# Streaming the moving operand of the float32r products alternately from its two halves

## The chip, the cores and the metric

The kernel runs on one core of a Trainium2 chip. The metric is the device time of one execution in microseconds (us), first instruction to last with what the program needs around them; lower is better. TensorE multiplies, VectorE (DVE) and ScalarE (ACT) read the results and prepare operands, SyncE (SP) and GpSimd (POOL) issue the transfers from memory.

## The reference, cut to what matters

A decoder block on 512 tokens of 1024 channels, in float32:

```python
h = _rmsnorm(x, norm_mix_g)
proj = h @ w_in                       # 1024 x 9216
p_a, p_b, q, p_g = jnp.split(proj, IN_SPLITS, axis=-1)
...
y_a = (gb * _causal_dwconv(gc * v, conv_a_w)) @ w_a_out
u = u * jax.nn.sigmoid(ug)
u = _causal_dwconv(u, conv_b_w) + conv_b_bias          # 31 taps
y_b = jax.nn.silu(_layernorm(u, ln_b_g, ln_b_b)) @ w_b_out
...                                   # 4 heads over 256 memory tokens: o
y_c = o @ w_att_out
merged = g[:, :, 0] * y_a + g[:, :, 1] * y_b + g[:, :, 2] * y_c
x = x + merged @ w_o
u = _causal_dwconv(_rmsnorm(x, norm_ffn_g) @ w_up, conv_ffn_w)
gt, up = jnp.split(u, 2, axis=-1)
x = x + (jax.nn.silu(gt) * up) @ w_down
out = _rmsnorm(x, norm_final_g)
```

## The kernel before, in words

**Products in three passes.** TensorE is fed float32r, a form of float32 that it streams in one pass but with fewer bits. So every operand is split into a high part (ACT casts it, `whi`, line 495 for weights) and a low part (DVE subtracts the high part from the source, `wlo`, line 499), and each product is three matmuls: high by high, high by low, low by high, summed in PSUM. Each matmul first loads a stationary operand of 128 columns (its own instruction, PEld in the profile) and then streams the moving operand, 256 or 512 columns, one after the other as they lie in SBUF.

**Seven products instead of eight.** The large products are formed by a scheme of Strassen's kind. A "quad" is one step of it for two blocks of 256 output channels: products 1, 2, 5, 6, 7, 3, 4 (`OPERAND`, line 553), each with sums or differences of weight blocks as its weights, gathered into banks a, b, c of PSUM and read out on the way (`quad_reads`, line 694, jobs r1 to r7). One product of a quad is 24 matmuls of 256 columns (`multiply`, line 663: weights stationary, the split activations `fb00`, `ft5` and so on moving). 18 quads make the input projection and 11 the up projection. So do the product with `w_o` (line 1598) and the down projection (`steps`, line 2051), with activations stationary and 512 columns of weights moving, through `product` (line 443). The three output products of the branches (`merge_product`, line 1407) stream 512 columns of activations; keys and scores stream 256, values and weighted sums 512.

Counted from the code: 29 quads x 7 x 24 + 192 (keys) + 96 (scores) + 66 (end of the down projection) = 5226 float32r matmuls of 256 columns, and 1319 of 512, of which two (the channel mean, line 1297) do not pass through a changed line.

**Who sets the order.** PE's order is written out by hand (`seq`, lines 1771 to 1885). Every other engine's order comes from `Jobs.run` (line 229): each job has an engine, an estimated cost, the jobs it comes after and the buffers it takes. The due time of a job is worked out backwards from the estimated costs of the PE jobs (`MM`, `MM_HALF`, `MM_QUAD`, line 419, us for a matmul), moved by two tables of offsets (`LATER`, `AHEAD`), and among the ready jobs the one with the earliest start and due time is emitted next. The split weights lie in a ring of four buffers (`UNIT_BUFS`), the raw ones in six.

**Readers of the banks.** With PSUM columns in the order of the tokens, or of the output channels, ACT and DVE read a bank from front to back: `quad_reads` (lines 702 to 724), the keys (838), values (896, 904), exponentials (1082), attention output (1133, 1138), gates (`weigh`, 1451), the rows after `w_o` (`add_row`, 1629) and after the down projection (`read`, `read_end`, 2073, 2084). The reading r7 is a scalar_tensor_tensor (`minus`, line 452), which gives -a - s.

Of the kernel before, what the change touches and what calls it, by code (L numbers as in the profile page):

```python
# [331 lines left out]
def hybrid_block_kernel(  # L332
# [83 lines left out]
        return n / 1160.0 + 0.175 + extra  # L416

    TAP = 0.665
    MM, MM_HALF, MM_QUAD = 0.2268, 0.12, 0.1142
    LOAD, MORE, MORE_WIDE = 1.42, 2.55, 2.55  # L420
    LOAD_LATENCY, MORE_LATENCY = 3.1, 3.4

# [17 lines left out]
    nc.scalar.dma_start(out=pk[:, :N_GAINS], in_=packed[:, :N_GAINS])  # L440
    nc.scalar.copy(mean_w, mean_col.broadcast_to([P, P]))

    def product(ps, w_hi, w_lo, s_hi, s_lo, start, stop, again=False):


        nc.tensor.matmul(ps, s_hi, w_hi, start=start, stop=False, skip_group_check=again)  # L446
        nc.tensor.matmul(ps, s_hi, w_lo, start=False, stop=False, skip_group_check=again)  # L447
        nc.tensor.matmul(ps, s_lo, w_hi, start=False, stop=stop, skip_group_check=again)  # L448
# [214 lines left out]
    def multiply(q, f, act):  # L663
        if f in (1, 2, 5):
            make(("bank", q, BANK_OF[f]))
        ps = halves(("bank", q, BANK_OF[f]))
        (w_hi, w_lo), (hi, lo) = w_units.pop((q, f)), form[act, OPERAND[f]]
        for c in range(2):
            at = slice(c * P, (c + 1) * P)
            for i in range(4):  # L670
                k = 3 - i if f == 4 and c else i
                first = f in (1, 2, 5) and i == 0 and c == 0
                again = not (f in (1, 2, 5) and c == 0)
                for n, (w, a) in enumerate(((w_hi, hi), (w_hi, lo), (w_lo, hi))):
                    nc.tensor.matmul(  # L675
                        ps[:, c, :], w[:, k, at], a[k], start=first and n == 0,
                        stop=i == 3 and n == 2, skip_group_check=again,
                    )

# [14 lines left out]
    def quad_reads(q, first, second, ring, after=()):  # L694

        f, s = lambda: two(first), lambda: two(second)
        bank = lambda b: ("bank", q, b)
        view = lambda b: halves(bank(b))

        def read1():  # L700
            make(first)
            nc.scalar.copy(f()[:, :, lo_t], view("a"))

        def read5():
            make(second)
            nc.scalar.copy(s()[:, :, hi_t], view("b"))

        def add(t, b):
            nc.vector.tensor_tensor(t, t, b, op=ALU.add)

        job(("r1", q), "ACT", actv(512), read1, [(q, 1)] + list(after),
            take=[(first, ring)], use=[bank("a")])
        job(("r2", q), "DVE", dve(512), lambda: add(f()[:, :, lo_t], view("c")),
            [(q, 2), ("r1", q)], use=[bank("c"), first])
        job(("r5", q), "ACT", actv(512), read5, [(q, 5)] + list(after),
            take=[(second, ring)], use=[bank("b")])
        job(("r6", q), "ACT", actv(512), lambda: nc.scalar.copy(f()[:, :, hi_t], view("a")),
            [(q, 6), ("r1", q)], use=[bank("a"), first])
        job(("r7", q), "DVE", dve(512), lambda: minus(s()[:, :, hi_t], view("a"), s()[:, :, hi_t]),
            [(q, 7), ("r5", q)], use=[bank("a"), second])  # L720
        job(("r3", q), "DVE", dve(512), lambda: add(f()[:, :, hi_t], view("b")),
            [(q, 3), ("r6", q)], use=[bank("b"), first])
        job(("r4", q), "ACT", actv(512), lambda: nc.scalar.activation(
            s()[:, :, lo_t], view("a"), AF.Copy, scale=-1.0), [(q, 4), ("r5", q)],
            use=[bank("a"), second])

    def ready_of(q, second):
# [101 lines left out]
    for h in range(HEADS):  # L829
        for g in range(2):  # L830
            if h or g:
                unit_job(("K", h, g), block(w_kv, h * 256, g))

        def keys_scaled(h=h):
            make(("kt", h))
            t = tiles["kt", h][:, :512].rearrange("p (c n) -> p c n", c=2)
            row = tiles["rm",][:, :N_MEM].unsqueeze(1).broadcast_to([P, 2, N_MEM])
            nc.vector.tensor_tensor(t, halves(("bank", "K", h)), row, op=ALU.mult)
# [49 lines left out]
    for hp in range(2):  # L888
        for kp in range(4):
            if hp or kp:  # L890
                unit_job(("V", hp, kp), w_v[hp, kp], 2)
        for c in range(MC):
            def values_high(hp=hp, c=c):
                if c == 0:
                    make(("vh", hp), F32R)
                nc.scalar.activation(
                    two(("vh", hp))[:, c, :], tiles["bank", "V", hp, c], AF.Copy,
                    scale=R_MEM[:, c : c + 1],
                )

            def values_low(hp=hp, c=c):
                if c == 0:
                    make(("vl", hp), F32R)
                nc.vector.scalar_tensor_tensor(
                    two(("vl", hp))[:, c, :], tiles["bank", "V", hp, c], R_MEM[:, c : c + 1],
                    two(("vh", hp))[:, c, :].bitcast(F32), op0=ALU.mult, op1=ALU.subtract,
                )

            new = lambda s: [((s, hp), ANY)] if c == 0 else []
            old = lambda s: [] if c == 0 else [(s, hp)]  # L910
            job(("vh", hp, c), "ACT", scaled_act(512), values_high,
                [("V", hp, 3), ("m", "scale")] + ([("vh", hp, 0)] if c else []), take=new("vh"),
                use=[("bank", "V", hp, c)] + old("vh"))
            job(("vl", hp, c), "DVE", TAP, values_low,
                [("vh", hp, c)] + ([("vl", hp, 0)] if c else []), take=new("vl"),
                use=[("bank", "V", hp, c), ("vh", hp)] + old("vl"))

    def keys_product(h, g, ks):
# [6 lines left out]
        for j in range(2):  # L925
            at, again = slice(j * P, (j + 1) * P), j > 0
            for k in ks:
                for n, (w, a) in enumerate(((w_hi, m_hi), (w_hi, m_lo), (w_lo, m_hi))):
                    nc.tensor.matmul(  # L929
                        ps[:, j, :], w[:, k, at], a[:, k, :],  # L930
                        start=first and j == 0 and k == 0 and n == 0,
                        stop=g == 1 and k == 3 and n == 2, skip_group_check=again,
                    )
# [117 lines left out]
    for h in range(HEADS):  # L1051
# [18 lines left out]
        for tp in range(2):  # L1070
# [7 lines left out]
            def exps(h=h, tp=tp, top=top, den=den, bank=bank):  # L1078
                if tp == 0:
                    make(("pr", h))  # L1080
                for i in range(2):
                    nc.scalar.activation(
                        four(("pr", h))[:, 2 * tp + i, :], halves(bank)[:, i, :], AF.Exp,
                        bias=top[:, i : i + 1], accum_out=den[:, i : i + 1],
                    )

# [38 lines left out]
        for d in range(2):  # L1125
# [4 lines left out]
            def o_high(h=h, d=d, bank=bank):  # L1130
                if d == 0:
                    make(("oh", h), F32R)
                nc.scalar.copy(two(("oh", h))[:, d, :], tiles[bank])

            def o_low(h=h, d=d, bank=bank):
                if d == 0:
                    make(("ol", h), F32R)
                nc.vector.tensor_tensor(
                    two(("ol", h))[:, d, :], tiles[bank], two(("oh", h))[:, d, :].bitcast(F32),
                    op=ALU.subtract,  # L1140
                )

            job(("oh", h, d), "ACT", actv(512), o_high,
# [263 lines left out]
    def merge_product(br, m, g):  # L1407
        w_hi, w_lo = w_units.pop(("merge", br, m, g))
        for j in range(2):
# [2 lines left out]
            at = slice(j * P, (j + 1) * P)  # L1412
            for i in range(4):
                k = 4 * g + i
                hi, lo = (two((s, k // 2))[:, k % 2, :] for s in PARTS[br])
                first, last = k == 0, k == KC - 1
                nc.tensor.matmul(ps, w_hi[:, i, at], hi, start=first, stop=False)  # L1417
                nc.tensor.matmul(ps, w_hi[:, i, at], lo, start=False, stop=False)  # L1418
# [13 lines left out]
    for br in (2, 0, 1):  # L1432
        for m in range(4):
# [14 lines left out]
            for j in range(2):  # L1448
                def weigh(j=j, br=br, m=m, gate=gate):
                    t = two(gate)[:, j, :]  # L1450
                    nc.vector.tensor_tensor(t, tiles["bank", "y", br, m, j], t, op=ALU.mult)

                job(("weigh", br, m, j), "DVE", dve(512), weigh,
                    [("merge", br, m, 1), ("sigmoid", br, m)],
# [170 lines left out]

    def add_row(p, t):
        for r, h, sign in WO_READ[p]:
            row = two(("x1", 2 * r + t))[:, h, :]
            nc.vector.tensor_tensor(
                row, row, tiles["bank", "wo", wo_bank(p), t],  # L1630
                op=ALU.add if sign > 0 else ALU.subtract,
            )

# [435 lines left out]

    def read(p, t):  # L2070
        for r, h, sign in READ[p]:
            row = late["x1"][2 * r + t][h]
            nc.vector.tensor_tensor(
                row, row, tiles["bank", chain(p), t],
                op=ALU.add if sign > 0 else ALU.subtract,
            )

    def read_end(i):
# [5 lines left out]
        nc.vector.tensor_tensor(row, row, src, op=ALU.add)  # L2084

    def square(t, h, cols=slice(0, SEQ), into=None):
        nc.scalar.activation(
# [149 lines left out]
```

## Time and profile before

| What | Value |
|---|---|
| time, 3 runs | 925.33 us median (925.14 to 925.72) |
| span of the profiled execution | 923.8 us; its own time is not listed apart, and the median of the runs is 1.5 us above the span |
| PE, PEld busy | 916.6 us (6677 matmuls), 862.8 us |
| DVE, ACT, POOL busy | 837.4, 671.0, 126.5 us |
| granted TensorE clock, mean | 0.999 |
| DMA | 190.60 MB, mean 206 GB/s |

How to read the profile: busy time counts an instruction from its start to its end. Matmuls overlap, so the busy time of PE says that it always had one in flight, not how fast they went; for that the distance from one start to the next is read from the timeline, or a piece of the chain is divided by its count. The chain is followed back from the last instruction to what released it, step by step. In a group of instructions "idle before" is time that the engine stood still ahead of them, with what ended it. Tile names stand without buffer numbers: `bank<-fb10h,whi` is a matmul that writes a PSUM bank from the moving operand `fb10h` and the stationary `whi`.

### The profile page before, as it was taken

Reading aid. Unit: us, or ns where it says so; the run is one execution under the profiler, and the core shown is the slowest. Engines: PE = TensorE matmul, PEld = TensorE weight load, DVE = VectorE, ACT = ScalarE, POOL = GpSimd, SP = SyncE. Lnnn points to the kernel's source line nnn. Section 1 sums busy time; section 2 is a strip of 40 time slices with the busy share of each in tenths; the row PEclk is TensorE's granted clock in tenths of the full one; section 3 lists DMA queues with packets and bytes.
Section 4 is the critical chain, followed back from the end, with each engine's and each line's share of the span. In section 5 each row is a group of like instructions: output and inputs, shape, how many; then the busy total and the mean of one; then the engine's idle time right before and its main releaser. Section 6 shows DMA issues by size and latency. Waiting matters only on the chain.

```text
span 923.8 us, 16764 instructions
## 1 busy us (share of the span) xinstructions
PE 916.6 (99%) x6677; PEld 862.8 (93%) x6677; DVE 837.4 (91%) x953; ACT 671.0 (73%) x911; POOL 126.5 (14%) x153
## 2 busy tenths in 40 slices
PE   9999999999999999999999999999999999999997
PEld 8999999999989999999899888899999999988886
DVE  6897999989989999999986779898999889999987
ACT  7567988879977887788746743777766676765656
POOL 0121121101111211110100001021221121003300
PEclk9999999999999999999999999999999999999999
DMA  9999689666787879788956598499999877789962
GB/s 364 367 252 199 151 178 205 167 160 137 194 188 205 183 168 213 174 210 201 220 108 173 157 322 187 114 227 307 279 248 226 207 142 149 197 266 338 244 131 92
DMA packets 54366, 190.60 MB, mean 206 GB/s; under 512 B 6160, under 2 KB 6544, under 8 KB 54288
## 3 DMA queue, kind: packets, MB, share of 16 engines
q0 software_dynamic: 20880, 75.24, 45.2%
q1 hardware_dynamic: 33120, 114.02, 34.7%
q8 instruction: 52, 0.85, 0.3%
q10 hardware_dynamic: 288, 0.27, 0.1%
q14 instruction: 26, 0.21, 0.1%
HBM read 185.31 MB, written 4.19 MB: 205 GB/s over the span
## 4 chain that ended last, share of the span: by engine, by line
PE 95%; DMA 2%; DVE 1%; issue 0%; ACT 0%; POOL 0%; DVEq 0%; POOLq 0%; ACTq 0%
PE bank L675 57%; PE bank L448 7%; PE bank L446 7%; PE bank L447 7%; PE bank L1418 5%; PE bank L1417 5%; PE bank L1419 5%; PE bank L929 2%; DMA wf<-in_w_up 2%; PE bank L1766 0%; PE ss L802 0%; DVE wlo L499 0%; PE bank L1166 0%; DVE upc L1373 0%; DVE gtc L1373 0%
## 5 line engine op out<-in xcount | busy, mean ns | idle before, releaser
L495 ACT CAST whi<-wf 128x1024 fp32r<-128x1024 f32 (+1 forms) x199 | 206.9, 1044 | 97.7 <-PE bank L675 39.3
L499 DVE TENSOR_TENSOR wlo<-wf,whi 128x1024 fp32r<-128x1024 f32 (+1 forms) x193 | 232.4, 1211 | 29.8 <-ACT whi L495 29.6
L1238 ACT ACTIVATE tp<-u,pk 128x510 f32<-128x510 f32 (+22 forms) x184 | 119.4, 704 | 7.0 <-DVE acc L1245 6.9
L1245 DVE TENSOR_TENSOR acc<-acc,tp 128x1020 f32<-128x1020 f32 (+22 forms) x92 | 109.2, 1188 | 6.0 <-ACT tp L1238 5.0
L633 POOL DMA_DIRECT2D wf<-in_w_in x51 | 45.1, 890 | 245.1 <-DVE wlo L499 160.2
L675 PE MATMUL bank<-ft6h,wlo 128*128 128x256 f32 x232 | 64.3, 277 | 0.1
L675 PE MATMUL bank<-fb10h,whi 128*128 128x256 f32 x232 | 64.4, 278 | 0.0
L675 PE MATMUL bank<-fb00h,whi 128*128 128x256 f32 x232 | 64.4, 278 | 0.0
L675 PE MATMUL bank<-ft6h,whi 128*128 128x256 f32 x232 | 64.4, 277 | 0.0
L675 PE MATMUL bank<-ft7h,whi 128*128 128x256 f32 x232 | 64.3, 277 | 0.0
L675 PE MATMUL bank<-ft7l,whi 128*128 128x256 f32 x232 | 64.3, 277 | 0.0
L675 PE MATMUL bank<-ft7h,wlo 128*128 128x256 f32 x232 | 64.3, 277 | 0.0
L675 PE MATMUL bank<-fb00l,whi 128*128 128x256 f32 x232 | 64.3, 277 | 0.0
L675 PE MATMUL bank<-fb11h,whi 128*128 128x256 f32 x232 | 64.3, 277 | 0.0
L675 PE MATMUL bank<-fb00h,wlo 128*128 128x256 f32 x232 | 64.3, 277 | 0.0
L675 PE MATMUL bank<-ft5h,wlo 128*128 128x256 f32 x232 | 64.3, 277 | 0.0
L675 PE MATMUL bank<-ft5h,whi 128*128 128x256 f32 x232 | 64.3, 277 | 0.0
L675 PE MATMUL bank<-ft5l,whi 128*128 128x256 f32 x232 | 64.3, 277 | 0.0
L675 PE MATMUL bank<-ft6l,whi 128*128 128x256 f32 x232 | 64.2, 277 | 0.0
L675 PE MATMUL bank<-fb10h,wlo 128*128 128x256 f32 x232 | 64.2, 277 | 0.0
L675 PE MATMUL bank<-fb10l,whi 128*128 128x256 f32 x232 | 64.2, 277 | 0.0
L675 PE MATMUL bank<-fb11l,whi 128*128 128x256 f32 x232 | 64.1, 276 | 0.0
(388 smaller groups left out, 3146.1 us busy)
## 6 DMA issues: line engine op xcount, KB each, us to landing
wf<-in_w_in SPq DMA_DIRECT2D x55, 512.0 KB, 5.1
wf<-in_w_in POOLq DMA_DIRECT2D x51, 512.0 KB, 6.2
wf<-in_w_up SPq DMA_DIRECT2D x29, 512.0 KB, 5.7
wf<-in_w_up POOLq DMA_DIRECT2D x28, 512.0 KB, 6.1
wf<-in_w_down SPq DMA_DIRECT2D x15, 512.0 KB, 3.7
wf<-in_w_att_out SPq DMA_DIRECT2D x8, 512.0 KB, 4.5
wf<-in_w_a_out SPq DMA_DIRECT2D x8, 512.0 KB, 4.2
wf<-in_w_b_out SPq DMA_DIRECT2D x8, 512.0 KB, 4.3
```

The source lines that it names most:

```text
L446: nc.tensor.matmul(ps, s_hi, w_hi, start=start, stop=False, skip_group_check=again)
L447: nc.tensor.matmul(ps, s_hi, w_lo, start=False, stop=False, skip_group_check=again)
L448: nc.tensor.matmul(ps, s_lo, w_hi, start=False, stop=stop, skip_group_check=again)
L495: nc.scalar.copy(parts[0], src())
L499: nc.vector.tensor_tensor(lo, src(), hi.bitcast(F32), op=ALU.subtract)
L633: nc.gpsimd.dma_start(out=tiles[key], in_=block(w, col[c], k), accum_op=ALU.add)
L675: nc.tensor.matmul(ps[:, c, :], w[:, k, at], a[k], start=first and n == 0, stop=i == 3 and n == 2, skip_group_check=again,)
L1238: nc.scalar.activation(two(("tp", p, s))[:, j, s:], two(("u", p))[:, j, : SEQ - s], AF.Copy, scale=weight(j),)
L1245: nc.vector.tensor_tensor(a, a, two(("tp", p, s))[:, :, s:], op=ALU.add)
L1417: nc.tensor.matmul(ps, w_hi[:, i, at], hi, start=first, stop=False)
L1418: nc.tensor.matmul(ps, w_hi[:, i, at], lo, start=False, stop=False)
L1419: nc.tensor.matmul(ps, w_lo[:, i, at], hi, start=False, stop=last)
```

## The change

A view `in_turns` is put on the moving operand of every float32r product except the channel mean. It splits the columns into two halves and runs through them alternately: 0, n/2, 1, n/2+1 and so on. Addresses follow each other no longer at a step of 4 bytes, but jump by half the operand (512 bytes for 256 columns, 1024 for 512) and back. The result therefore lies in PSUM with its columns mixed: column 2i is old column i, column 2i+1 is old column i + n/2. Each reader of such a bank takes PSUM through `turned` (a step of two floats, first the even columns, then the odd ones) and writes, or reads its second operand, through `parted`, which only splits the contiguous side in two so that the shapes agree. What lies in SBUF is as before. Readers of banks that no such product writes (transposes, the row of norms) stay as they are.

Two small things go with it. r7 becomes a subtraction `s - a` on tensor_tensor, for which r5 now writes the negated bank (ACT activation with scale -1 in place of a copy). And the planner's costs for a matmul are lowered.

```diff
-    MM, MM_HALF, MM_QUAD = 0.2268, 0.12, 0.1142
+    MM, MM_HALF, MM_QUAD = 0.2158, 0.114, 0.1119
...
+    def in_turns(t):
+        return t.rearrange("p (a b) -> p b a", a=2)
+
+    def turned(t):
+        if len(t.shape) == 3:
+            return t.rearrange("p c (b a) -> p c a b", a=2)
+        return t.rearrange("p (b a) -> p a b", a=2)
+
+    def parted(t):
+        if len(t.shape) == 3:
+            return t.rearrange("p c (a b) -> p c a b", a=2)
+        return t.rearrange("p (a b) -> p a b", a=2)
...
     def product(ps, w_hi, w_lo, s_hi, s_lo, start, stop, again=False):
+        w_hi, w_lo = in_turns(w_hi), in_turns(w_lo)
         nc.tensor.matmul(ps, s_hi, w_hi, start=start, stop=False, skip_group_check=again)
...
                     nc.tensor.matmul(
-                        ps[:, c, :], w[:, k, at], a[k], start=first and n == 0,
+                        ps[:, c, :], w[:, k, at], in_turns(a[k]), start=first and n == 0,
...
-            nc.scalar.copy(f()[:, :, lo_t], view("a"))
+            nc.scalar.copy(parted(f()[:, :, lo_t]), turned(view("a")))
...
-            nc.scalar.copy(s()[:, :, hi_t], view("b"))
+            nc.scalar.activation(
+                parted(s()[:, :, hi_t]), turned(view("b")), AF.Copy, scale=-1.0)
-        def add(t, b):
-            nc.vector.tensor_tensor(t, t, b, op=ALU.add)
+        def add(t, b, op=ALU.add):
+            nc.vector.tensor_tensor(parted(t), parted(t), turned(b), op=op)
...
-        job(("r7", q), "DVE", dve(512), lambda: minus(s()[:, :, hi_t], view("a"), s()[:, :, hi_t]),
+        job(("r7", q), "DVE", dve(512), lambda: add(s()[:, :, hi_t], view("a"), ALU.subtract),
...
-                hi, lo = (two((s, k // 2))[:, k % 2, :] for s in PARTS[br])
+                hi, lo = (in_turns(two((s, k // 2))[:, k % 2, :]) for s in PARTS[br])
...
-                    nc.vector.tensor_tensor(t, tiles["bank", "y", br, m, j], t, op=ALU.mult)
+                    nc.vector.tensor_tensor(
+                        parted(t), turned(tiles["bank", "y", br, m, j]), parted(t), op=ALU.mult)
```

The keys' matmuls (line 929) get `in_turns` in the same way, and the other readers listed above get `turned` and `parted` in the same way.

With the new costs the planner puts jobs in another order. PE's instructions keep theirs, one for one. The lists of the two kernels differ by 344 lines for DVE (of 903), 253 for ACT (733), 28 for POOL (150) and 30 for SP (226); a moved line counts twice.

More of the change, by code (lines that the diff above doesn't have):

```diff
@@ L716, in quad_reads @@
             take=[(second, ring)], use=[bank("b")])
-        job(("r6", q), "ACT", actv(512), lambda: nc.scalar.copy(f()[:, :, hi_t], view("a")),
+        job(("r6", q), "ACT", actv(512), lambda: nc.scalar.copy(
+            parted(f()[:, :, hi_t]), turned(view("a"))),
             [(q, 6), ("r1", q)], use=[bank("a"), first])
-        job(("r7", q), "DVE", dve(512), lambda: minus(s()[:, :, hi_t], view("a"), s()[:, :, hi_t]),
+        job(("r7", q), "DVE", dve(512), lambda: add(s()[:, :, hi_t], view("a"), ALU.subtract),
             [(q, 7), ("r5", q)], use=[bank("a"), second])
@@ L723, in quad_reads @@
         job(("r4", q), "ACT", actv(512), lambda: nc.scalar.activation(
-            s()[:, :, lo_t], view("a"), AF.Copy, scale=-1.0), [(q, 4), ("r5", q)],
+            parted(s()[:, :, lo_t]), turned(view("a")), AF.Copy, scale=-1.0), [(q, 4), ("r5", q)],
             use=[bank("a"), second])
@@ L837, in keys_scaled @@
             row = tiles["rm",][:, :N_MEM].unsqueeze(1).broadcast_to([P, 2, N_MEM])
-            nc.vector.tensor_tensor(t, halves(("bank", "K", h)), row, op=ALU.mult)
+            nc.vector.tensor_tensor(
+                parted(t), turned(halves(("bank", "K", h))), parted(row), op=ALU.mult)
         def keys_high(h=h):
@@ L896, in values_high @@
                 nc.scalar.activation(
-                    two(("vh", hp))[:, c, :], tiles["bank", "V", hp, c], AF.Copy,
+                    parted(two(("vh", hp))[:, c, :]), turned(tiles["bank", "V", hp, c]), AF.Copy,
                     scale=R_MEM[:, c : c + 1],
@@ L904, in values_low @@
                 nc.vector.scalar_tensor_tensor(
-                    two(("vl", hp))[:, c, :], tiles["bank", "V", hp, c], R_MEM[:, c : c + 1],
-                    two(("vh", hp))[:, c, :].bitcast(F32), op0=ALU.mult, op1=ALU.subtract,
+                    parted(two(("vl", hp))[:, c, :]), turned(tiles["bank", "V", hp, c]),
+                    R_MEM[:, c : c + 1], parted(two(("vh", hp))[:, c, :].bitcast(F32)),
+                    op0=ALU.mult, op1=ALU.subtract,
                 )
@@ L929, in keys_product @@
                     nc.tensor.matmul(
-                        ps[:, j, :], w[:, k, at], a[:, k, :],
+                        ps[:, j, :], w[:, k, at], in_turns(a[:, k, :]),
                         start=first and j == 0 and k == 0 and n == 0,
@@ L1082, in exps @@
                     nc.scalar.activation(
-                        four(("pr", h))[:, 2 * tp + i, :], halves(bank)[:, i, :], AF.Exp,
+                        parted(four(("pr", h))[:, 2 * tp + i, :]), turned(halves(bank)[:, i, :]),
+                        AF.Exp,
                         bias=top[:, i : i + 1], accum_out=den[:, i : i + 1],
@@ L1132, in o_high @@
                     make(("oh", h), F32R)
-                nc.scalar.copy(two(("oh", h))[:, d, :], tiles[bank])
+                nc.scalar.copy(parted(two(("oh", h))[:, d, :]), turned(tiles[bank]))
             def o_low(h=h, d=d, bank=bank):
@@ L1138, in o_low @@
                 nc.vector.tensor_tensor(
-                    two(("ol", h))[:, d, :], tiles[bank], two(("oh", h))[:, d, :].bitcast(F32),
-                    op=ALU.subtract,
+                    parted(two(("ol", h))[:, d, :]), turned(tiles[bank]),
+                    parted(two(("oh", h))[:, d, :].bitcast(F32)), op=ALU.subtract,
                 )
@@ L1450, in weigh @@
                     t = two(gate)[:, j, :]
-                    nc.vector.tensor_tensor(t, tiles["bank", "y", br, m, j], t, op=ALU.mult)
+                    nc.vector.tensor_tensor(
+                        parted(t), turned(tiles["bank", "y", br, m, j]), parted(t), op=ALU.mult)
                 job(("weigh", br, m, j), "DVE", dve(512), weigh,
@@ L1627, in add_row @@
         for r, h, sign in WO_READ[p]:
-            row = two(("x1", 2 * r + t))[:, h, :]
+            row = parted(two(("x1", 2 * r + t))[:, h, :])
             nc.vector.tensor_tensor(
-                row, row, tiles["bank", "wo", wo_bank(p), t],
+                row, row, turned(tiles["bank", "wo", wo_bank(p), t]),
                 op=ALU.add if sign > 0 else ALU.subtract,
@@ L2071, in read @@
         for r, h, sign in READ[p]:
-            row = late["x1"][2 * r + t][h]
+            row = parted(late["x1"][2 * r + t][h])
             nc.vector.tensor_tensor(
-                row, row, tiles["bank", chain(p), t],
+                row, row, turned(tiles["bank", chain(p), t]),
                 op=ALU.add if sign > 0 else ALU.subtract,
@@ L2083, in read_end @@
             row, src = row[:, ENDS[i]], tiles[end_banks[i]][:, :256]
-        nc.vector.tensor_tensor(row, row, src, op=ALU.add)
+        nc.vector.tensor_tensor(parted(row), parted(row), turned(src), op=ALU.add)
     def square(t, h, cols=slice(0, SEQ), into=None):
```

## The prediction

> **What bounds the kernel now.** I read the page's busy times first, then the chain, then the waits of each engine, and only then single instructions.
>
> ```profile
> span 923.8 us, 16764 instructions
> PE 916.6 (99%) x6677; PEld 862.8 (93%) x6677; DVE 837.4 (91%) x953; ACT 671.0 (73%) x911; POOL 126.5 (14%) x153
> PE 95%; DMA 2%; DVE 1%; issue 0%; ACT 0%; POOL 0%; DVEq 0%; POOLq 0%; ACTq 0%
> ```
>
> PE is the bound: 95% of the chain that ended last is PE. But DVE has only 86 us free (923.8 - 837.4), so it is the next bound, and near. The waits say which of the two runs ahead:
>
> ```profile
> PE bank L1766 <- POOL ident masks.py:199: 1.4, 1, 1.4
> ACT whi L495 <- PE bank L675: 53.8, 50, 1.9
> DVE wlo L499 <- ACT whi L495: 43.9, 40, 3.9
> ```
>
> The first row is all that PE waits for. ACT waits 53.8 us for PE to give back buffers of split weights, and DVE waits for ACT behind it: the producers are ahead and the ring of four is full. So the time is the number of matmuls by the distance between their starts. That distance comes from long pieces of the chain (start, length, count) and from a timeline of the down projection (first and last of 15 matmuls):
>
> ```profile
> 62.83 103.59 PE bank L675 x912
> 285.83 153.12 PE bank L675 x1344
> 643.39 160.88 PE bank L675 x1414
> 187.61 2.83 PE bank L675 x24
> 841.80 0.39 PE L448 MATMUL bank<-whi,zl 128*128 128x512 f32 x1
> ...
> 844.97 0.39 PE L447 MATMUL bank<-wlo,zh 128*128 128x512 f32 x1
> ```
>
> 256 columns: 417.59 us / 3670 = 113.8 ns. Some short stretches are slower: 2.83 us / 24 = 117.9 ns. 512 columns: 3.17 us / 14 = 226.4 ns, double that of 256, so nearly all of it is paid per column, 0.442 ns. Is that the array or its supply? The start of the kernel tells, where PE is still slow:
>
> ```profile
> 1.73 3.62 PE L1766 MATMUL bank<-ident 128*128 128x128 f32 x16
> 6.62 0.41 PE L929 MATMUL bank<-ml,whi 128*128 128x256 f32 x1
> 6.83 0.41 PE L929 MATMUL bank<-mh,wlo 128*128 128x256 f32 x1
> 7.04 0.33 PE L929 MATMUL bank<-mh,whi 128*128 128x256 f32 x1
> 7.21 0.28 PE L929 MATMUL bank<-ml,whi 128*128 128x256 f32 x1
> 7.32 0.28 PE L929 MATMUL bank<-mh,wlo 128*128 128x256 f32 x1
> 177.49 1.04 PE L1166 MATMUL bank<-ident,pr 128*128 128x128 f32 x8
> ```
>
> Until 7.04 the same 256 columns take 0.21 us, then 0.11: the rate of the array doubles there (the page shows the granted clock at full already, so I read this from the spacing). The 16 matmuls with the identity lie (3.62 - 0.42) / 15 = 213.3 ns apart (a last one lasts about 0.42 us, as estimated from the 0.41 us rows), the transposes at full rate, 128 columns too, (1.04 - 0.28) / 7 = 109 ns (0.28 us for a last one, as at 7.21): half, plus 2 to 3 ns, of which I take 3. float32r does not halve so well. At half rate 256 columns take 0.42 / 2 = 0.21 us; if it is 213 ns as for the identity, 0.833 ns a column, full rate would be 0.417 ns a column, and 0.442 are seen. **So about one clock in 17 is lost at full rate only, in proportion to columns:** something that supplies the columns is 6% too slow. That is what reading in turns can touch.
>
> **The change part by part.**
>
> *512 columns.* 1317 of them change. Without the loss: 512 x 0.417 + 3 = 216.3 ns, 10.1 ns less: 1317 x 10.1 = 13.3 us. No row shows an alternating read, so the bounds are the 226.4 ns of today and 213.3 ns without any fixed part, and I take 216.3, since both the identity and the transposes stream at the array's own rate.
>
> [...]
>
> *256 columns.* The array alone would need 256 x 0.417 + 3 = 109.7 ns, but each matmul has a load of 128 columns too. Matmuls of a single moving column show what loads alone cost:
>
> ```profile
> 20.23 1.70 PE L802 MATMUL ss<-mean_col,msq 128*128 128x1 f32 x14
> L802 PE MATMUL ss<-mean_col,msq x16: 164/250/250, 20.1 to 21.7; 128*128 128x1 f32 x16
> ```
>
> (1.70 - 0.25) / 13 = 111.5 ns. The load becomes the limit; I take 112 ns and save 1.8 ns: 5226 x 1.8 = 9.4 us (bounds 0 and 2.3 ns, 12.0 us). For the stretches at 117.9 ns I add 1.5 us, between nothing and about 4 (estimate: if they are a fifth of the 5226, 1045 x 4.1 ns).
>
> *Readers.* 159 DVE and 144 ACT instructions now read PSUM with a step of two floats, their element counts as before. Neighbouring rows:
>
> ```profile
> L709 DVE TENSOR_TENSOR gt<-gt,bank 128x512 f32<-128x512 f32 x22 | 15.0, 682 | 2.9 <-PE bank L675 2.9
> L452 DVE SCALAR_TENSOR_TENSOR uu<-bank,uu 128x512 f32<-128x512 f32 x11 | 7.5, 683 | 1.8 <-PE bank L675 1.8
> L1735 DVE TENSOR_TENSOR z<-upc,gtc 128x1024 f32<-128x1024 f32 x11 | 13.4, 1217 | 0.2
> L723 ACT ACTIVATE uu<-bank 128x512 f32<-128x512 f32 x11 | 6.5, 588 | 0.0
> L706 ACT COPY uu<-bank 128x512 f32<-128x512 f32 x11 | 6.4, 580 | 0.9 <-PE bank L675 0.9
> ```
>
> r7 costs the same on either form (683 and 682 ns), r5 gains 8 ns x 29, 0.2 us on ACT. No row reads with a step, so the price lies between nothing and one more slot per element, 1217 - 682 = 535 ns on DVE, 159 x 0.535 = 85 us. Reading in one operand from PSUM, in the other from SBUF costs per element already what two reads from SBUF cost (682 for 512, 1217 for 1024: 1.04 ns for each further one), so the engine's own pace sets it, and I take nothing.
>
> *Order.* The planner moves jobs on DVE, ACT, POOL and SP; PE keeps its order. I cost this at nothing: what hides it is the full ring of weights (ACT's 53.8 us of waiting). Without that cover PE would stall by what a late unit takes, about 1.05 to 1.2 us each.
>
> *Where a faster PE meets the next bound.* Three stretches (us, then PE, PEld, DVE, ACT, POOL busy), and the middle of the second:
>
> ```profile
> 0.00:43.00 43.00, 41.64 (x270) 38.43 (x271) 32.94 (x49) 29.69 (x40) 2.18 (x10) 1.00 0.98 362
> 597.00:645.00 48.00, 47.87 (x401) 47.17 (x400) 42.34 (x49) 35.29 (x50) 9.49 (x11) 1.00 0.99 264
> 820.00:880.00 60.00, 60.00 (x269) 49.63 (x269) 59.86 (x64) 36.72 (x42) 15.68 (x18) 1.00 1.04 297
> 608.24 1.06 ACT whi L495
> 610.57 8.41 DMA wf<-in_w_up
> 619.54 11.44 DMA wf<-in_w_up x2
> 643.39 1.63 PE bank L675 x12
> ```
>
> From 0 to 43 us the transfers run full (0.98), so half of what PE gains there goes: about 0.5 us. From 608 to 643 the chain leaves PE for transfers, ACT and DVE; PE comes back to it at 643.39 and cannot be earlier: some 376 matmuls x 1.8 ns = 0.7 us. From 820 to 880 DVE has 0.14 us free: the 2.6 us gained on some 260 matmuls of 512 columns are lost. Together 3.9 us. Elsewhere DVE's 86 us of free time, less what PE gains, are the cover.
>
> **Sum:** 13.3 + 9.4 + 1.5 - 3.9 = 20.3 us. Span 923.8 - 20.3 = 903.5; with the 1.5 us by which the median of the runs stands above the span, **905 us**.
>
> **The rivals.**
>
> *DVE holds PE back (912 to 920 us).* DVE is also full from 100 to 180 and from 300 to 440 us:
>
> ```profile
> 100.00:180.00 80.00, 80.00 (x704) 80.00 (x704) 79.70 (x96) 68.77 (x106) 12.88 (x15) 1.00 0.80 183
> 300.00:440.00 140.00, 140.00 (x1230) 139.79 (x1229) 139.11 (x148) 114.73 (x157) 21.63 (x25) 1.00 0.82 193
> ```
>
> If its work there cannot be put off, the gain of some 1930 matmuls is lost as well (3.5 us), and if the new order brings weights late some ten times, 10 us more: about 916. Against it: part of that work is convolution taps without a near due time.
>
> *The lost clock belongs to the column count.* If it comes every 16 columns whatever the address, nothing changes but the order: 925 us.
>
> *Reading PSUM with a step is slow.* The mechanism on the other side. At DVE's readers, two slots per element add 85 us: 837 + 85 = 922 us of work, and DVE cannot be without gaps: at the start (32.94 of 43 us busy) and around 597 to 645 (42.34 of 48) it stands for 16 us, and elsewhere too, so about 950 us. It decides from some 0.3 us a reading on (86 us free, less 35 us of gaps that stay as an estimate, over 159). Against it: the pace of 1.04 ns above.
>
> *Alternating reads are slower for PE.* If each column costs another clock, 256 columns take the 0.21 us of the half rate and 512 twice that: 5226 x 0.1 + 1317 x 0.2 = 786 us more, about 1710 us. Any part of it makes the kernel slower. Against it: a loss of one clock in 17 read in order shows the supply comes in pieces of about 16 columns, and two halves need as many pieces.
>
> [...] No run here shows a strided read so far.
>
> **How the numbers follow.** Forecast 897 to 912 us, 0.70. DVE holds, 912 to 920: 0.10. No change, 925: 0.05. Slow readers, 950: 0.08. Slower PE, 1000 to 1710: 0.07. With all PE terms at their bounds, 17.3 (1317 x 13.1 ns) + 12.0 + 4 = 33.3 us, and 3.9 us lost, the time is 923.8 - 29.4 + 1.5 = 896 us. From there to 920 the range takes in the first two cases, 8 in 10. A measurement of this kernel tells about 0.2% from no change: faster 0.80, same 0.05, slower 0.15.
>
> **What would show it.** In the profile after: matmuls of 512 columns near 216 ns apart (at 226 the lost clock stayed), of 256 near 112 (at 109.7 the load was no limit); L709's successor at 682 ns (not 1217); PE's waits still a few us, DVE full from the up projection's end on. I am wrong if PE's spacing grows, if readers lengthen, or if PE shows new waits for `wlo` of more than some 5 us.

## The result, and the profile after

The changed kernel takes 904.08 us (median of four runs, 903.81 to 904.52), the kernel before 925.24 us beside it (925.01 to 925.72): a ratio of 0.9769, with a 95% interval of 0.9755 to 0.9783. That is 21.2 us, or 2.3%, less. The span of the profiled execution fell from 923.8 to 902.6 us.

The head of the page after (span, busy times, shares of the chain):

```profile
span 902.6 us, 16777 instructions
PE 889.7 (99%) x6677; PEld 849.6 (94%) x6677; DVE 836.0 (93%) x953; ACT 666.7 (74%) x911; POOL 126.4 (14%) x153
PE 28%; DVE 5%; DMA 2%; issue 2%; ACT 1%; DVEq 0%; POOLq 0%; ACTq 0%
```

PE is busy for 26.9 us less, DVE and ACT nearly as long as before (1.4 and 4.3 us less). The shares of the chain must be read with care here: they add up to 38%, because the chain could be followed back only to 568 us. That PE has 28% of the span in it says nothing about the first 568 us. So the distances between matmuls have to be read again, 256 columns from a long piece of the chain and 512 columns from the timeline of the down projection (first and last of 16 neighbours):

```profile
627.56 158.16 PE bank L692 x1414
788.31 2.68 PE bank L692 x24
```

```profile
854.64 0.38 PE L465 MATMUL bank<-whi,zl 128*128 128x512 f32 x1
...
857.88 0.38 PE L465 MATMUL bank<-whi,zl 128*128 128x512 f32 x1
```

256 columns: 158.16 / 1414 = 111.9 ns, and 2.68 / 24 = 111.7 where the kernel before had stretches of 117.9. 512 columns: 3.24 / 15 = 216.0 ns. The readers of the banks, from the groups by line with shapes kept apart (busy us, mean ns, then idle time ahead):

```profile
L727 DVE TENSOR_TENSOR gt<-gt,bank 128x512 f32<-128x512 f32 x22 | 14.9, 682 | 2.7 <-PE bank L692 2.7
L723 ACT ACTIVATE uu<-bank 128x512 f32<-128x512 f32 x11 | 6.6, 596 | 0.0
L735 ACT COPY gt<-bank 128x512 f32<-128x512 f32 x11 | 6.4, 580 | 0.7
```

A reading with a step of two floats takes 682 ns on DVE, to the nanosecond what a reading in order took. On ACT, 580 ns for a copy is the old figure too. The row of 596 ns is r5, which was a copy of 580 ns and now changes the sign as well.

What is new is that PE waits. The six longest of PE's waits in the profile after (waited for: us in total, times, longest us; five shorter ones have 1.2 us together), and then two rows of the other engines:

```profile
PE bank L692 <- DVE wlo L516: 1.5, 3, 0.8
PE bank L1789 <- POOL ident masks.py:199: 1.4, 1, 1.4
PE bank L692 <- DVE g L727: 1.0, 2, 0.8
PE bank L464 <- DVE wlo L516: 0.6, 1, 0.6
PE bank L463 <- DVE x L2096: 0.6, 1, 0.6
PE bank L465 <- DVE zl L1952: 0.4, 1, 0.4
```

```profile
ACT whi L512 <- PE bank L692: 44.9, 40, 1.8
DVE wlo L516 <- ACT whi L512: 30.8, 30, 2.7
```

Before, the row for `ident` was all. Now DVE releases PE in five of these six rows. ACT's wait for buffers went from 53.8 to 44.9 us and DVE's behind it from 43.9 to 30.8: the producers are still ahead for most of the time, but by less. Where they are not, the windows tell (us, then busy time and instructions of PE, PEld, DVE, ACT and POOL):

```profile
100.00:180.00 80.00, 79.89 (x713) 79.51 (x713) 77.84 (x93) 66.34 (x103) 12.07 (x14) 1.00 0.82 182
300.00:440.00 140.00, 138.58 (x1198) 136.96 (x1197) 137.63 (x146) 112.60 (x155) 21.59 (x25) 1.00 0.82 193
820.00:880.00 60.00, 58.75 (x271) 50.65 (x270) 57.58 (x60) 36.81 (x43) 13.65 (x16) 1.00 0.94 221
800.00:860.00 60.00, 58.13 (x272) 49.67 (x271) 59.90 (x64) 35.54 (x42) 15.64 (x18) 1.00 1.04 298
```

From 820 to 880 us PE was busy for the whole 60 us before and now has 1.25 us without a matmul in flight; from 300 to 440 us it has 1.4. Since the kernel has by then gained some 20 us, the work that lay from 820 to 880 us before now lies from 800 to 860 (64 instructions on DVE both times). There DVE has 0.1 us free, and PE is without a matmul for 1.87 us.

To set the 21.2 us against terms I took, in both traces, the distance from each matmul's start to the next one of the same column count (5198 and 1296 of them). Distances over 1.25 times the median count as stalls, with what they have above the median; the mean is that of the others.

```
                          before      after      difference
256 columns, mean         114.43 ns   111.66 ns  2.77 ns x 5226 = 14.5 us
512 columns, mean         227.51 ns   215.88 ns  11.63 ns x 1317 = 15.3 us
stalls of PE              3.2 us      10.4 us    -7.2 us
sum                                              22.6 us   (span: 21.2 us)
```

The remaining 1.4 us must lie in what this count does not cover (transposes, changes between column counts, the ends of the kernel).

### The profile page after: what moved, and what is told of

Same layout as the page of the kernel before. It is cut to its first block, busy times and chain, and to the rows that moved or that the text cites. A ratio compares the mean times of both kernels' runs of the same rounds, so it can differ in the third digit from the quotient of the medians.

```text
span 902.6 us, 16777 instructions
## 1 busy us (share of the span) xinstructions
PE 889.7 (99%) x6677; PEld 849.6 (94%) x6677; DVE 836.0 (93%) x953; ACT 666.7 (74%) x911; POOL 126.4 (14%) x153
## 5 line engine op out<-in xcount | busy, mean ns | idle before, releaser
L512 ACT CAST whi<-wf 128x1024 fp32r<-128x1024 f32 (+1 forms) x203 | 210.5, 1044 | 86.4 <-PE bank L692 30.0
L516 DVE TENSOR_TENSOR wlo<-wf,whi 128x1024 fp32r<-128x1024 f32 (+1 forms) x197 | 236.9, 1210 | 21.0 <-ACT whi L512 20.7
L1260 ACT ACTIVATE tp<-u,pk 128x507 f32<-128x507 f32 (+22 forms) x184 | 119.6, 706 | 4.0 <-DVE acc L1267 2.2
L1267 DVE TENSOR_TENSOR acc<-acc,tp 128x1022 f32<-128x1022 f32 (+22 forms) x92 | 109.1, 1187 | 3.1 <-ACT tp L1260 1.4
L650 POOL DMA_DIRECT2D wf<-in_w_in x55 | 48.3, 879 | 251.6 <-DVE wlo L516 164.8
L692 PE MATMUL bank<-fb11h,wlo 128*128 128x256 f32 x232 | 63.8, 275 | 0.0
```

Source lines behind the costliest of these rows:

```text
L512: nc.scalar.copy(parts[0], src())
L516: nc.vector.tensor_tensor(lo, src(), hi.bitcast(F32), op=ALU.subtract)
L650: nc.gpsimd.dma_start(out=tiles[key], in_=block(w, col[c], k), accum_op=ALU.add)
L692: nc.tensor.matmul(ps[:, c, :], w[:, k, at], in_turns(a[k]), start=first and n == 0, stop=i == 3 and n == 2, skip_group_check=again,)
L1260: nc.scalar.activation(two(("tp", p, s))[:, j, s:], two(("u", p))[:, j, : SEQ - s], AF.Copy, scale=weight(j),)
L1267: nc.vector.tensor_tensor(a, a, two(("tp", p, s))[:, :, s:], op=ALU.add)
```

## The experiments

Each run is compared with runs of the kernel before that were made beside it, with medians of 925.75 us (the first four kernels), 925.49 us (e5 to e8) and 925.9 us (e9 to e12).

### Which products gain: 512 columns alone, 256 columns alone

e1 turns only the operands of 512 columns, with `turned` and `parted` at their readers alone; r5 and r7 are those of the changed kernel. Against the kernel before:

```diff
-    MM, MM_HALF, MM_QUAD = 0.2268, 0.12, 0.1142
+    MM, MM_HALF, MM_QUAD = 0.2158, 0.12, 0.1142
...
+        if w_hi.shape[-1] == 512:
+            w_hi, w_lo = in_turns(w_hi), in_turns(w_lo)
```

> Only the matmuls of 512 columns read in turns; those of 256 and the readers of their banks stay as before, and the planner gets the old costs for 256. Theory, the gain is the sum of two terms on PE: 512 columns 216 ns apart, 256 columns 114.4 ns on average as before, so about 1317 x 11.6 ns = 15 us of the 21 us come with this part, less what PE then waits: 910 to 913 us. Rival, the order of the planner brings the gain and not the reading: the distances do not follow the shape, and the time is near 925 or near 904.

Measured: 914.0 us (913.5 to 914.08), ratio 0.9869 [0.9854, 0.9883]. The chain and the timeline of e1:

```profile
634.08 161.13 PE bank L693 x1416
```

```profile
841.74 0.38 PE L465 MATMUL bank<-wlo,zh 128*128 128x512 f32 x1
...
844.97 0.38 PE L465 MATMUL bank<-wlo,zh 128*128 128x512 f32 x1
```

256 columns stay at 161.13 / 1416 = 113.8 ns, 512 columns are at 3.23 / 15 = 215.3 ns here (215.84 over all). The gain of 11.8 us is made of 11.67 ns x 1317 = 15.4 us for 512 columns, 2.4 us for 256 (a mean of 113.97 ns in place of 114.43) and 4.6 us that go to stalls (7.8 us in place of 3.2); some 1.4 us are not assigned. The distances follow the shape, as the theory had it; the time lies 1.0 us above its range.

e2 starts from the changed kernel and takes the turns away from the operands of 512 columns and from their readers:

```diff
-    MM, MM_HALF, MM_QUAD = 0.2158, 0.114, 0.1119
+    MM, MM_HALF, MM_QUAD = 0.2268, 0.114, 0.1119
...
-        w_hi, w_lo = in_turns(w_hi), in_turns(w_lo)
+        if w_hi.shape[-1] == 256:
+            w_hi, w_lo = in_turns(w_hi), in_turns(w_lo)
```

> Only the matmuls of 256 columns read in turns. Theory: 256 columns 111.7 ns apart throughout, the slower stretches near 118 ns gone, 512 columns 227 ns; 5226 x 2.75 ns = 14 us of gain at most, less new waits: 911 to 915 us. Rival A, the load of the stationary operand is not the limit at 256 columns: 109.7 ns and 905 us. Rival B, the slower stretches come from the 512-column part: they stay, and the time is 916 to 918 us.

Measured: 916.59 us (915.77 to 918.14), ratio 0.99 [0.9884, 0.9916]. The timeline of e2, and its window of the down projection:

```profile
841.67 0.39 PE L466 MATMUL bank<-whi,zl 128*128 128x512 f32 x1
...
845.07 0.39 PE L466 MATMUL bank<-whi,zl 128*128 128x512 f32 x1
```

```profile
820.00:880.00 60.00, 58.85 (x259) 48.12 (x258) 59.97 (x62) 35.60 (x41) 15.71 (x18) 1.00 1.06 291
```

512 columns are back at 3.40 / 15 = 226.7 ns, 256 columns at 111.65 ns over all, and no distance of 117 to 121 ns is left. The distances came out as the theory had them, the time 1.6 us above its range. It lies in the range of rival B, but B's reason is excluded, since the slower stretches are gone. Instead PE's stalls are 9.2 us here, 6 more than before (in the profiled run, the slowest of the four), and the window shows PE without a matmul for 1.15 us while DVE has 0.03 us free. The gains of the two halves of the change, 1.31% and 1.00%, add up to the 2.31% of the whole. That is partly luck: e1 also gains 2.4 us at 256 columns, and e1 and e2 together have 10.6 us of new stalls where the whole change has 7.2.

### What the order is worth

e3 is the kernel before with nothing but the new planner costs, e4 the changed kernel with the old ones:

```diff
# e3
-    MM, MM_HALF, MM_QUAD = 0.2268, 0.12, 0.1142
+    MM, MM_HALF, MM_QUAD = 0.2158, 0.114, 0.1119
# e4
-    MM, MM_HALF, MM_QUAD = 0.2158, 0.114, 0.1119
+    MM, MM_HALF, MM_QUAD = 0.2268, 0.12, 0.1142
```

> The kernel before with the new planner costs and nothing else. Theory: PE's distances stay at 113.4 and 226.7 ns, and with a full ring of weights the order is worth little: 924 to 927 us. Rival, the new order is part of the gain: below 920 us.

> The changed kernel with the old planner costs. Theory: PE's distances as in the changed kernel (111.7 and 215.9 ns), and only the new waits of PE (10 us in the changed kernel) differ, since the planner holds PE for slower than it is: 903 to 908 us. Rival, the planner must know the faster PE: more waits for weights, above 910 us.

Measured: e3 927.47 us (926.4 to 929.09), ratio 1.0019 [1.0009, 1.0028]; e4 905.53 us (904.57 to 905.88), ratio 0.9777 [0.9762, 0.9791]. Distances in e3 are those of before (114.44 and 227.50 ns), in e4 those of after (111.66 and 215.88). The new costs lose 1.7 us on the kernel before; on the changed kernel their interval overlaps the one without them. So the order explains none of the gain, and with the faster matmuls its effect is too small to be told.

### Two runs by single columns, and other ways to read

The clock lost in 17 is the prediction's estimate (0.442 ns a column seen, 0.417 worked out from the half rate), and a supply in pieces is its explanation, which no trace shows. If it holds, other ways through the same columns should tell what such a supply minds. e5 and e6 keep the readers consistent (DVE and ACT then write, or read, SBUF in another pattern). e5 reads first the even, then the odd columns, so each address is 8 bytes after the last; e6 runs through four quarters in turn:

```diff
# e5, in in_turns
-        return t.rearrange("p (a b) -> p b a", a=2)
+        return t.rearrange("p (b a) -> p a b", a=2)
# e6, in in_turns, turned and parted
-        ... a=2)
+        ... a=4)
```

> As the changed kernel, but the moving operand is read first in its even columns, then in its odd ones (a step of two floats, no jumps between halves); the readers of the banks alternate between the two halves of a bank instead of stepping by two. Theory L, a clock is lost whenever the reading comes to the next 64 bytes without something in between: 64 bytes now last 8 columns, so the loss doubles, 120 ns for 256 columns and 240 ns for 512, about 950 to 960 us. Rival S, only a reading at a step of one float loses clocks: 111.7 and 215.9 ns, about 904 us.

> The operand is read in turns from its four quarters; the readers of the banks step by four floats. Both theories: PE 111.7 and 215.9 ns apart, as with two halves. The readers: theory, DVE's and ACT's pace does not depend on the step, 682 and 587 ns for 512 elements, and the time is 902 to 906 us. Rival, a step of 16 bytes in PSUM costs the readers: over 800 ns, and above 910 us.

Measured: e5 1822.34 us, ratio 1.9687 [1.9657, 1.9716]; e6 1149.36 us, ratio 1.2415 [1.2396, 1.2433]. Timelines of the down projection, and the same reading by DVE as above, e5 first:

```profile
1699.52 0.63 PE L463 MATMUL bank<-whi,zh 128*128 128x512 f32 x1
...
1706.29 0.63 PE L463 MATMUL bank<-whi,zh 128*128 128x512 f32 x1
```

```profile
L727 DVE TENSOR_TENSOR gt<-gt,bank 128x512 f32<-128x512 f32 x22 | 15.0, 686 | 52.3 <-PE bank L692 52.3
```

And e6:

```profile
1049.83 0.45 PE L464 MATMUL bank<-wlo,zh 128*128 128x512 f32 x1
...
1054.08 0.45 PE L464 MATMUL bank<-wlo,zh 128*128 128x512 f32 x1
```

```profile
L727 DVE TENSOR_TENSOR gt<-gt,bank 128x512 f32<-128x512 f32 x22 | 15.0, 687 | 14.0 <-PE bank L692 13.9
```

451.3 ns for 512 columns with a step of two floats, 283.3 ns with four quarters. What I expected of PE fell in both: e5 is near neither 240 nor 216, e6 not near 216. The part on the readers held, 686 and 687 ns. In the last column of the groups one sees DVE standing still for PE, for 52.3 us ahead of this line alone in e5.

e7 and e8 take pieces of 2 and of 16 columns from the halves in turn. They put the same pattern on the PSUM output, so that the result lies in order and the readers are those of before:

```diff
+    def in_turns(t):
+        return t.rearrange("p (a b c) -> p b a c", a=2, c=2)    # e8: c=16
...
+        ps, w_hi, w_lo = in_turns(ps), in_turns(w_hi), in_turns(w_lo)
...
-                        ps[:, c, :], w[:, k, at], a[k], start=first and n == 0,
+                        in_turns(ps[:, c, :]), w[:, k, at], in_turns(a[k]), start=first and n == 0,
```

> Pieces of two columns are taken in turns from the two halves, and PE writes its result back into the bank in the old order by the same pattern on the output, so that all readers stay as before. Theory L: the 64 bytes of each half still alternate, so 111.7 and 215.9 ns, and 902 to 907 us with less change than the changed kernel. Rival W, writing PSUM out of order costs PE: above 113 and 227 ns, 925 us or more.

> Pieces of 16 columns (64 bytes) are taken in turns from the two halves, with the same pattern on the output; readers as before. Theory L1, what costs is coming to new 64 bytes at all after 16 columns: the loss stays, 113.4 and 226.7 ns, 924 to 927 us. Theory L2, what costs is that the next 64 bytes are the neighbouring ones: the loss is gone, 111.7 and 215.9 ns, 903 to 907 us.

Measured: e7 1329.31 us, ratio 1.4359 [1.4337, 1.438]; e8 970.54 us, ratio 1.0487 [1.0469, 1.0504]. The timelines, e7 and then e8:

```profile
1229.53 0.50 PE L452 MATMUL bank<-whi,zl 128*128 128x512 f32 x1
...
1234.45 0.50 PE L452 MATMUL bank<-whi,zl 128*128 128x512 f32 x1
```

```profile
884.62 0.40 PE L450 MATMUL bank<-whi,zh 128*128 128x512 f32 x1
...
888.22 0.40 PE L450 MATMUL bank<-whi,zh 128*128 128x512 f32 x1
```

328.0 and 240.0 ns. Theory L fell for e7, and both theories for e8; e7's time would fit rival W. But here two things had changed at once, the reading and the writing. e9 and e10 are e7 and e8 without `in_turns(ps)`: only the moving operand is read so, and the columns stay mixed in the banks.

> Pieces of two columns are taken in turns from the two halves, on the moving operand alone: PE writes its banks front to back again, and the readers do not sort the columns back, so the output has its columns and rows mixed. Against e7 this leaves out the pattern on the output. Theory, the output's pattern was what cost in e7: 216 and 112 ns, near 905 us. Rival, the reading itself costs where two neighbouring columns are followed by a jump: the 328 and 165 ns of e7 stay, near 1325 us.

> Pieces of 16 columns in turns, on the moving operand alone, the columns not sorted back. Theory, in e8 one clock of the two lost per 16 columns is the reading's and one the output's: 226.7 and 113.4 ns, near 925 us. Rival R, both are the reading's: 240 and 120 ns, near 969 us. Rival Z, both are the output's: 216 and 112 ns, near 905 us.

Measured in one run each: 1330.95 and 971.84 us. The timelines, e9 and then e10:

```profile
1229.74 0.50 PE L450 MATMUL bank<-whi,zh 128*128 128x512 f32 x1
...
1234.66 0.50 PE L450 MATMUL bank<-whi,zh 128*128 128x512 f32 x1
```

```profile
884.76 0.40 PE L452 MATMUL bank<-whi,zl 128*128 128x512 f32 x1
...
888.36 0.40 PE L452 MATMUL bank<-whi,zl 128*128 128x512 f32 x1
```

Again 328.0 and 240.0 ns, so the rivals on the reading hold in both: the whole loss is the reading's, and the pattern on the PSUM output costs nothing that can be seen. Whether it would cost something at 216 ns, with no slower reading to hide it, no run shows.

e11 asks whether the halves must be far apart. Single columns come in turns from two neighbouring runs of 16 columns, 64 bytes apart instead of 512 or 1024; the readers are those of before:

```diff
-        return t.rearrange("p (a b) -> p b a", a=2)
+        return t.rearrange("p (c a b) -> p c b a", a=2, b=16)
```

> Single columns in turns as in the changed kernel, but from neighbouring runs of 16 columns (64 bytes apart) instead of the two halves; on the moving operand alone, the columns not sorted back. Theory, it is enough that successive columns come from two runs of 64 bytes: 216 and 112 ns, near 905 us, as with the halves. Rival, the distance matters, and neighbours this close get in each other's way: above 226.7 and 113.4 ns, up to the 451 and 230 ns of the step of two floats, 930 to 1820 us.

Measured in one run: 904.39 us. The timeline of e11:

```profile
854.72 0.38 PE L452 MATMUL bank<-whi,zl 128*128 128x512 f32 x1
...
857.96 0.38 PE L452 MATMUL bank<-whi,zl 128*128 128x512 f32 x1
```

3.24 / 15 = 216.0 ns, as with halves. For 512 columns it does not matter whether the two runs lie 64 or 1024 bytes apart; nothing between was tried.

### Where the rest of the gain went

e12 is the changed kernel with less work on DVE: the convolution adds its taps only for the last 64 tokens, and two of the sums ahead of the down projection are cut.

```diff
-                a = two(("acc", p))[:, :, s:]
-                nc.vector.tensor_tensor(a, a, two(("tp", p, s))[:, :, s:], op=ALU.add)
+                a = two(("acc", p))[:, :, 448:]
+                nc.vector.tensor_tensor(a, a, two(("tp", p, s))[:, :, 448:], op=ALU.add)
...
-        z00, z01, z10, z11 = (quarter(r, c, ps) for r in range(2) for c in range(2))
+        z00, z01, z10, z11 = (quarter(r, c, ps)[:, :, :16] for r in range(2) for c in range(2))
...
-                y_u(), y_u(), x_u(), op=ALU.add), [("xa", u), ("wl", ("pd", "d", u))]))
+                y_u()[:, :64], y_u()[:, :64], x_u()[:, :64], op=ALU.add), [("xa", u), ("wl", ("pd", "d", u))]))
```

> The changed kernel with DVE's sums cut short: the additions of convolution taps made by ACT run over the last 64 tokens only, those of y_sum over 64 columns, those of z over 16 tokens of each quarter, so the output is not the reference's; order and planner costs are the same. DVE loses about 115 us of work. Theory, the 7 us that the changed kernel lost against the pure gain of PE are waits for DVE between 100 and 440 us and between 780 and 880 us: they go, 897 to 899 us. Rival, they come from transfers, ACT or the order: 902 us or more.

Measured: 900.02 us (898.76 to 901.26), ratio 0.9725 [0.9709, 0.9741]. The windows of e12, and PE's two longest waits beside the one for `ident`:

```profile
300.00:440.00 140.00, 140.00 (x1204) 138.46 (x1203) 115.56 (x148) 114.20 (x156) 21.80 (x26) 1.00 0.83 196
...
820.00:880.00 60.00, 60.00 (x290) 52.93 (x288) 49.28 (x61) 37.40 (x43) 12.19 (x14) 1.00 0.88 204
```

```profile
PE bank L465 <- DVE zl L1952: 0.4, 1, 0.4
PE bank L692 <- ACT gt L719: 0.3, 1, 0.3
```

Compare these with the rows of the changed kernel: DVE is busy for 749.2 us in all, 87 less (115 were expected); from 300 to 440 us it had 2.4 us free and now has 24.4, and PE has no time without a matmul any more, nor from 820 to 880. Stalls fall from 10.4 to 5.5 us, and the ratio by 0.0044, 4.1 us; the two intervals do not overlap. The distances between matmuls are as in the changed kernel (111.66 and 215.88 ns). By stretch, the stalls from 100 to 180 and from 300 to 440 us fall from 2.9 to 0.3 us, those from 180 to 300 from 1.2 to 0.5, those from 780 to 880 from 3.0 to 0.7. From 440 to 645 us they go only from 2.6 to 2.4. So the greater part of what the change lost to stalls was lost to DVE, and not all of it; the time lies 1.0 us above the theory's range. Among the kernels that compute all of the reference, none was faster than the changed one; e4 cannot be told from it.

## Why the prediction was right, and where its sizes were off

905 us were predicted and 904.08 measured, and the time fell for the reason that was given. The steps, one by one:

**512 columns, 13.3 us.** Right in kind, slightly too small: 15.3 us. The distance after is 215.9 ns where 216.3 was taken. The larger part of the error lies in the distance before: 226.4 ns was read from one stretch of 15 matmuls, while the mean over all is 227.5, since some lie at 229 to 236. e1 shows the term by itself.

**256 columns, 9.4 + 1.5 us.** Undersized: 14.5 us. That the load of the stationary operand becomes the limit agrees with the distance, 111.66 ns: 112 was taken, matmuls of a single column had 111.5, and by the prediction's estimate the array alone would have given 109.7. No run changes the load by itself. The failed part of this term is the stretches at 117.9 ns, to which 1.5 us were given as a middle between 0 and 4. In the trace before, some 1060 of 5198 distances lie at 117 to 121 ns, so the estimate of a fifth was right and the whole of it was gained. e2 has none of them left and the changed kernel one. What they come from stays open. Counting distances of 116 ns or more, they come in long unbroken stretches: in the kernel before 105 from 285.7 us and 200 from 609.2 us. e3, where the other engines work in the new order, has 105 from 285.5 us and 200 from 609.0 us, and 1048 distances of 117 to 121 ns in all, so that order does not make them. e1 has 477, with the operands of 256 columns still read in order, so what PE does between them seems to matter.

**Readers at nothing.** Right: 682 ns on DVE before and after. The rival of slow readers is gone with that. The new form of r5 takes 16 ns more on ACT where 8 were forecast, some 0.5 us over 29 of them, on an engine that is not the bound.

**Order at nothing.** Nearly right: e3 loses 0.19% with the order alone, e4 shows no difference that can be told.

**Lost at the next bound, 3.9 us.** The right mechanism, but the sum was too small by nearly half, because stretches were left out: stalls grew by 7.2 us. By stretch (over all matmuls, changes of the column count included, so that the total is higher, 8.2 us) 0.3 us came from 0 to 43 us where 0.5 stood, 0.8 from 597 to 645 where 0.7 stood, and 2.9 from 800 to 860, where the work now lies that stood from 820 to 880 with 2.6. So the three stretches that were named came out nearly at their size. What was left out is the rest: 2.8 us from 100 to 180 and 300 to 440, 0.9 between them, 0.5 from 440 to 597. From 100 to 180 and from 300 to 440 us that is the rival in which DVE holds PE back. It took place there, with 2.8 us where it put 3.5, but without the 10 us for late weights that made up most of its price. e12 shows that it is DVE. PE's waits for `wlo` are 2.3 us in all, below the 5 us that were to count against the prediction.

**The sum.** Gains of 24.2 us were forecast and 29.8 came; 3.9 us of losses were forecast, and 7.2 us of stalls came with 1.4 that are not assigned. Gains and losses were both sized too small, by 5.6 and 4.7 us, and it is luck that the total came within 0.9 us.

**The rivals for PE.** The column count as the cause (925 us) is excluded by 215.9 ns for the same count. Slower alternating reads (up to 1710 us) did not come for two runs, but e5 shows that they were no idle worry: with a step of two floats the distance doubles, from 226.7 ns in order (e2) to 451.3, and the kernel takes 1822 us.

**The reason given against that rival** did not hold as it stood. It said that the supply comes in pieces of about 16 columns and that two halves need as many pieces. Pieces of 16 taken from two halves need as many too, and take 240.0 ns, not 216 or 227; four quarters take 283.3. A right number came from a picture that is too simple. The distances for 512 columns, as the timelines of the down projection give them:

```
way through the columns                       ns      ns per column
single columns from two halves (after)        216.0   0.422
single columns from two runs 64 bytes apart   216.0   0.422
in order (e2)                                 226.7   0.443
pieces of 16 from two halves                  240.0   0.469
single columns from four quarters             283.3   0.553
pieces of 2 from two halves                   328.0   0.641
even columns, then odd ones                   451.3   0.881
```

That single columns from two runs come at the pace estimated for the array (216.0 ns against 216.3) is shown; why it is so, and why two neighbouring columns from each half are half as dear again (328.0 ns), stays open. No run looked inside the supply.

## What to carry to other kernels

Divide a long piece of the chain by its count and compare it with the pace that the trace lets you estimate for the array (here 216.3 ns for 512 columns): this kernel, with PE 99% busy, still lost 5% at 512 columns to the way its operand was read (227.5 against 215.9 ns), and a view on the operand won it back. Try exactly the pattern that you mean to use, since its neighbours cost 5 to 97% here (970.54 to 1822.34 us against 925.49 before). When the bound engine becomes faster by a few per cent, count the stretches where the next engine is nearly full, every one of them: that is where most of the new stalls came here (DVE had 0.1 to 0.9 us free in stretches of 60 to 140 us).

## What the runs showed of the hardware that was not expected

- A float32r operand read with a step of two floats streams at half the pace (451.3 ns for 512 columns, 226.7 in order), while DVE and ACT read PSUM with the same step for nothing (682 ns on DVE, 580 on ACT for a copy).
- A matmul's pattern on its PSUM output, in pieces of 2 or of 16 columns, cost nothing beyond these slower readings: 328.0 and 240.0 ns with it and without it.
- Where single columns alternate, two runs need be no more than 64 bytes apart (216.0 ns), while four runs, the quarters, take 283.3 ns.
- In every kernel that reads 256 columns singly in turns from two runs the mean distance is 111.65 or 111.66 ns, next to the 111.5 ns of matmuls of a single column and above the 109.7 ns estimated for the array. The slow stretches of 117 to 121 ns, which the kernels that read these columns in order have (1059, 1048 and 477 distances), are gone there but for one.
